# Input projection by one level of Strassen's products, all of it first, in a hybrid mLSTM and conformer block

## The chip, the cores and the metric

The kernel runs on one core of one Trainium2 chip. The metric is the device time of one execution in microseconds. The times of before are those of three runs; the profile is one further execution, recorded by the hardware profiler. PE is the matrix engine, DVE, ACT and POOL the vector, scalar and GpSimd engines, SP the engine that issues most transfers.

## The reference

One layer on x of 1024 tokens by 1024 channels, all in float32:

```
proj = rmsnorm(x) @ w_in                  # 1024 x 7168
xa, za, ub, gb, zb, g_a, g_b = split(proj)  # seven sections of 1024 channels
xc = silu(conv4(xa));  q, k = blockdiag(xc);  v = blockdiag(xa)
ha = standardize(mlstm_chunkwise(q, k, v, gates(q, k, v)))       # 4 heads
ya = ((ha * g + skip * xc) * silu(za)) @ w_proj
c  = conv31(ub * sigmoid(gb))             # causal, per channel
yb = (silu(layernorm(c)) * silu(zb)) @ w_pw2 + b
x  = x + (sigmoid(g_a) * ya + sigmoid(g_b) * yb) @ w_out
x  = x + (p @ w_ple) * sigmoid(rmsnorm(x) @ w_gate)
out = rmsnorm(x)
```

## The kernel before

All activations lie with channels on the 128 partitions and tokens along the free axis, in 8 channel tiles of 128x1024. A float32 product is made of three passes in the engine's float32r format: each operand is split exactly in a high part (a cast, L87, on ACT) and a low part (a subtraction, L88, mostly on DVE), and hi x hi, hi x lo and lo x hi are added up in PSUM. `gemm` (L208 to 222) makes one output tile of 128 channels by 1024 tokens: 8 input tiles by 2 halves of the tokens by 3 passes, 48 matmuls of 128x512. `gemm_half` does one half with 24.

The input projection has 56 output tiles, 8 in each of seven sections: XA (input of the first branch), ZA (its gate), UB and GB (input and gate of the long conv), ZB, GA and GBT. Before, these tiles are mixed with the rest: XA with the short conv and v, ZA with the four heads of the matrix memory, GA with the projection of the first branch, GBT and ZB beside the layer norm of the second branch; then follow pw2, the merge, `out` and `gate`. So long chains of small operations have whole GEMMs of other tiles beside them.

Weights come through the class `Stream` (L137 to 175): a raw load on SP, a cast on ACT, a subtraction on DVE. The raw buffer `wr` is single, the split parts are double; raw tiles of `out` and `gate` go to ordinary slots, of which there are 20.

The long conv has 31 taps of 128x1024, each one instruction on DVE (L347, L350), in SBUF. `drain(n)` hands out a few of them after each piece of other work, with the scheduling priority CONV_LATER.

The order on each engine is written down once, when the program is built: a scheduler takes the instructions by priority and by when it expects their inputs. On the chip each engine runs its list in order and waits where an input is missing.

Of the kernel before, what the change touches and what calls it, by code (L numbers as in the profile page):

```python
# [45 lines left out]
def block_kernel(ctx: ExitStack, tc: tile.TileContext, xT, pT, w_in, w_proj, w_pw2, w_out, w_ple,  # L46
# [12 lines left out]
    pm = ctx.enter_context(tc.tile_pool(name="pm", bufs=4, space=bass.MemoryType.PSUM))
    dp = ctx.enter_context(tc.tile_pool(name="dp", bufs=1, space=bass.MemoryType.DRAM))  # L60

    uid = [0]

    def slot(shape=(P, S), dt=F32, pool=None):
        uid[0] += 1
        pool = pool or sp
        full = pool.tile([P, NCK // 2 * DV], dt, tag="s", name=f"s{uid[0]}")
# [10 lines left out]
    def mbank(n=512):  # L78
        uid[0] += 1
        return pm.tile([P, 512], F32, tag="m", name=f"m{uid[0]}")[:, :n]  # L80

    def gbank():
        uid[0] += 1
        return pg.tile([P, S], F32, tag="g", name=f"g{uid[0]}")

    def split(src, hi, lo, eng=V):
        A.copy(out=hi, in_=src)  # L87
        eng.tensor_tensor(out=lo, in0=src, in1=hi.bitcast(F32), op=ALU.subtract)  # L88

# [9 lines left out]
    x_t = []  # L99
    for t in range(NT):  # L100
        xt = slot()
        nc.sync.dma_start(out=xt, in_=xT[t * P:(t + 1) * P, :])
        x_t.append(xt)
    pools = [vp, vp, vp, vp, zp, zp, zp, sp]
    parts = [slot(dt=F32R, pool=q) for q in pools]
# [19 lines left out]
    G.memset(eps_c, EPS)  # L125

# [4 lines left out]
    ple_d = dp.tile([NT, P, S], F32, name="ple_d")  # L131
    c_d = dp.tile([NT, P, S], F32, name="c_d")
    ma_d = dp.tile([NT, P, S], F32, name="ma_d")
    mrow_d = dp.tile([NH, S + NCK], F32, name="mrow_d")

# [43 lines left out]

    def plan(kind, *cts):  # L180
        order.extend((kind, t) for t in cts)

    def plan_pair(t):
        plan("in", GB + t, UB + t)

    for t in range(NT):
        plan("in", XA + t)
        if t in (1, 4):
            plan_pair(t // 4)
    for h in range(NH):  # L190
        plan("in", ZA + 2 * h, ZA + 2 * h + 1)
        plan_pair(2 + h)
    for t in range(NT):
        plan("in", GA + t)
        plan("proj", t)
        if t in (0, 2):
            plan_pair(6 + t // 2)
    plan("in", *range(GBT, GBT + NT))
    plan("in", *range(ZB, ZB + NT))
    plan("pw2", *range(NT))  # L200
    for kind in ("out", "gate"):
        plan(kind, *range(NT))
        plan(kind, *range(NT))
    srcs = {"in": w_in, "proj": w_proj, "pw2": w_pw2, "out": w_out, "gate": w_gate}
# [3 lines left out]
    def gemm(kind, ct, act_hi, act_lo):  # L208
        """[128 output channels, 1024 tokens] = w tile^T @ act; act_*(kt, half)."""
# [30 lines left out]
    def rstd_cols(ssum, n, out):  # L240
        """out = 1/sqrt(ssum/D + eps), [128, n]"""
        rt = sm.tile([P, NCK], F32, tag="rt", name=f"rt{uid[0]}")
        uid[0] += 1
        A.activation(rt[:, :n], ssum, AF.Sqrt, bias=eps_c, scale=1.0 / D)
        V.reciprocal(out=out, in_=rt[:, :n])

    def row_bcast(dst, rcol, n):
        """dst [128, n*128] = every partition the values of rcol [128, n], token-major"""
        for c in range(n):
            PE.matmul(dst[:, c * P:(c + 1) * P], rcol[:, c:c + 1].broadcast_to([P, P]), ident,  # L250
                      start=True, stop=True)

# [1 line left out]

    def ple_tile(ct):
        ps = gbank()
        cs = slice(ct * P, (ct + 1) * P)
        for h in range(2):
            for k in range(2):
                o = ps[:, h * HT:(h + 1) * HT]  # L260
                hs = slice(h * HT, (h + 1) * HT)
                PE.matmul(o, wple_s[k][0][:, cs], p_s[k][0][:, hs], start=k == 0, stop=False)
                PE.matmul(o, wple_s[k][0][:, cs], p_s[k][1][:, hs], start=False, stop=False)
                PE.matmul(o, wple_s[k][1][:, cs], p_s[k][0][:, hs], start=False, stop=k == 1)
        st = slot()
        A.copy(out=st, in_=ps)  # L266
        G.dma_start(out=ple_d[ct], in_=st)

# [1 line left out]
    xsq = slot()  # L270
    with tc.manual_schedule(engines={mybir.EngineType.Activation}):
        for t in range(NT):
            sq = xsq if t == 0 else slot()
            A.activation(sq, x_t[t], AF.Square)
            if t > 0:
                V.tensor_tensor(out=xsq, in0=xsq, in1=sq, op=ALU.add)
            if t % 2 == 1:
                ple_tile(t // 2)
    ssq = mbank(2 * NCK)
    for c in range(NCK):  # L280
        PE.matmul(ssq[:, 2 * c:2 * c + 2], xsq[:, c * P:(c + 1) * P], ones2, start=True, stop=True)
    rx = sm.tile([P, NCK], F32, tag="rc", name="rx")
    rstd_cols(ssq.rearrange("p (c w) -> p c w", w=2)[:, :, 0], NCK, rx)
    for _ in range(2):
        ws.load()
        ws.prep()

    h_hi = [hp.tile([P, NT, HT], F32R, tag="H", name=f"hhi{h}") for h in range(2)]
    h_lo = [hp.tile([P, NT, HT], F32R, tag="H", name=f"hlo{h}") for h in range(2)]
    rrow = [mbank() for _ in range(2)]  # L290
    for h in range(2):
        row_bcast(rrow[h], rx[:, 4 * h:4 * h + 4], 4)
    for t in range(NT):
        for h in range(2):
            x = x_t[t][:, h * HT:(h + 1) * HT]
            V.scalar_tensor_tensor(out=x, in0=x, scalar=vcol("norm_g", t), in1=rrow[h],  # L296
                                   op0=ALU.mult, op1=ALU.mult)
            split(x, h_hi[h][:, t], h_lo[h][:, t], G if h else V)
# [562 lines left out]
```

## Time and profile before

| | us |
|---|---|
| median of three runs | 1172.96 |
| lowest and highest | 1172.73, 1173.2 |
| span of the profiled execution | 1169.3 |
| PE busy in it | 1147.2 |
| DVE busy in it | 817.7 |
| ACT busy in it | 400.4 |
| POOL busy in it | 33.0 |

The profiled span leaves out some 3.7 us that lie around it in a timed run (1173.0 less 1169.3). Matmuls overlap in the engine, so the busy time of one (some 0.39 us) is longer than the distance from one to the next, which is read from the count in a stretch of time.

### The profile page before, as it was taken

The page shows a single profiled execution, that of the slowest core. Times are in us where ns is not written, and L with a number is a line of the kernel's source. Part 1 is how long each engine was busy: PE and PEld are TensorE (multiplying, and loading weights), DVE is VectorE, ACT ScalarE, POOL GpSimd, SP SyncE. Part 2 cuts the span into 40 slices and gives each one's busy share as a digit, 9 for nine tenths or more (in the row PEclk, how much of TensorE's full clock was granted, in tenths as well). Part 3 has the DMA queues.
Part 4 walks back from the last instruction along what each step waited for, and adds up shares of the span by engine and source line. Part 5 has one row for each costly group of instructions (what it writes and reads, how often), then busy time and mean ns, then how long its engine had stood idle before and what let it go on. Part 6 is the DMA issues. An engine that isn't in the chain of part 4 may idle for free.

```text
span 1169.3 us, 13098 instructions
## 1 busy us (share of the span) xinstructions
PE 1147.2 (98%) x5276; PEld 929.8 (80%) x5276; DVE 817.7 (70%) x1113; ACT 400.4 (34%) x540; POOL 33.0 (3%) x67
## 2 busy tenths in 40 slices
PE   7999999999999999999999999999999999999996
PEld 5777777778787887888888888888888888888885
DVE  5929989869984699828769999365334545466875
ACT  7633323642525343221111111147232212334542
POOL 1400000000000000000000000000000000000000
PEclk9999999999999999999999999999999999999998
DMA  9311121201011011221211233211113229422232
GB/s 328 133 36 36 38 72 36 71 20 55 19 62 47 19 55 37 72 91 42 102 54 55 108 105 112 90 54 36 55 36 108 90 73 387 152 87 94 91 127 72
DMA packets 29660, 98.18 MB, mean 84 GB/s; under 512 B 3148, under 2 KB 5340, under 8 KB 29600
## 3 DMA queue, kind: packets, MB, share of 16 engines
q1 hardware_dynamic: 25344, 82.37, 20.5%
q0 software_dynamic: 4256, 14.98, 3.3%
q8 instruction: 41, 0.67, 0.2%
q14 instruction: 19, 0.16, 0.0%
HBM read 80.55 MB, written 16.79 MB: 83 GB/s over the span
## 4 chain that ended last, share of the span: by engine, by line
PE 93%; DVE 4%; ACT 1%; DMA 1%; issue 0%; SPq 0%; DVEq 0%; ACTq 0%
PE g L221 21%; PE g L217 21%; PE g L218 21%; PE g L235 5%; PE g L234 5%; PE g L236 5%; PE m L548 2%; PE m L561 2%; PE m L535 1%; PE m L403 1%; PE m L555 1%; PE m L512 1%; DVE s L296 1%; PE m L594 1%; PE m L421 1%; PE m L250 1%
## 5 line engine op out<-in xcount | busy, mean ns | idle before, releaser
L217 PE MATMUL g<-hhi,wh 128*128 128x512 f32 x896 | 354.4, 396 | 0.5 <-ACT s L266 0.5
L218 PE MATMUL g<-hlo,wh 128*128 128x512 f32 x896 | 352.2, 393 | 0.4 <-POOL hlo L88 0.4
L350 DVE SCALAR_TENSOR_TENSOR s<-s,vecs,s 128x1023 f32<-128x1023 f32 (+15 forms) x240 | 300.5, 1265 | 4.3
L221 PE MATMUL g<-hhi,wl 128*128 128x512 f32 x896 | 283.0, 394 | 0.0
L87 ACT CAST wh<-wr 128x1024 fp32r<-128x1024 f32 x72 | 75.8, 1053 | 437.1 <-PE g L218 432.4
L221 PEld LDWEIGHTS g<-hhi,wl 128*128 128x128 f32 x896 | 167.7, 188 | 38.3 <-issue 4.5
L217 PEld LDWEIGHTS g<-hhi,wh 128*128 128x128 f32 x896 | 168.3, 188 | 37.2 <-issue 2.9
L218 PEld LDWEIGHTS g<-hlo,wh 128*128 128x128 f32 x896 | 168.3, 188 | 36.2 <-issue 1.8
L88 DVE TENSOR_TENSOR wl<-wr,wh 128x1024 fp32r<-128x1024 f32 x72 | 87.9, 1220 | 121.4 <-ACT wh L87 121.2
L217 PE MATMUL g<-s,wh 128*128 128x512 f32 x256 | 101.0, 395 | 0.0
L218 PE MATMUL g<-s,wh 128*128 128x512 f32 x256 | 100.8, 394 | 0.0
L221 PE MATMUL g<-s,wl 128*128 128x512 f32 x256 | 80.2, 394 | 0.0
L87 ACT CAST wh<-s 128x1024 fp32r<-128x1024 f32 x32 | 33.6, 1050 | 76.8 <-PE g L235 32.6
L218 PEld LDWEIGHTS g<-s,wh 128*128 128x128 f32 x256 | 48.1, 188 | 11.4
L217 PEld LDWEIGHTS g<-s,wh 128*128 128x128 f32 x256 | 48.1, 188 | 11.3
L221 PEld LDWEIGHTS g<-s,wl 128*128 128x128 f32 x256 | 48.1, 188 | 11.3
L235 PE MATMUL g<-nlo,wh 128*128 128x512 f32 (+1 forms) x136 | 51.5, 379 | 0.0
L234 PE MATMUL g<-nhi,wh 128*128 128x512 f32 (+1 forms) x136 | 51.3, 377 | 0.0
L236 PE MATMUL g<-nhi,wl 128*128 128x512 f32 (+1 forms) x136 | 51.2, 377 | 0.0
L88 DVE TENSOR_TENSOR wl<-s,wh 128x1024 fp32r<-128x1024 f32 x32 | 39.1, 1223 | 16.1 <-ACT wh L87 16.0
L235 PE MATMUL g<-mlo,wh 128*128 128x512 f32 x128 | 50.0, 391 | 0.0
L234 PE MATMUL g<-mhi,wh 128*128 128x512 f32 x128 | 49.8, 389 | 0.0
(193 smaller groups left out, 1340.7 us busy)
## 6 DMA issues: line engine op xcount, KB each, us to landing
wr<-in_w_in SPq DMA_DIRECT2D x56, 512.0 KB, 3.4
s<-in_xT SPq DMA_DIRECT2D x16, 512.0 KB, 9.1
s<-in_w_out SPq DMA_DIRECT2D x16, 512.0 KB, 10.1
s<-in_w_gate SPq DMA_DIRECT2D x16, 512.0 KB, 3.5
ple_d<-s POOLq DMA_DIRECT2D x8, 512.0 KB, 3.8
c_d<-s POOLq DMA_DIRECT2D x8, 512.0 KB, 2.9
wr<-in_w_proj SPq DMA_DIRECT2D x8, 512.0 KB, 3.4
s<-c_d SPq DMA_DIRECT2D x8, 512.0 KB, 4.0
```

What stands on the lines that cost most here:

```text
L87: A.copy(out=hi, in_=src)
L88: eng.tensor_tensor(out=lo, in0=src, in1=hi.bitcast(F32), op=ALU.subtract)
L217: PE.matmul(o, hi[:, kt], act_hi(kt, h), start=kt == 0, stop=False)
L218: PE.matmul(o, hi[:, kt], act_lo(kt, h), start=False, stop=False)
L221: PE.matmul(o, lo[:, kt], act_hi(kt, h), start=False, stop=kt == NT - 1)
L234: PE.matmul(ps, hi[:, kt], act_hi(kt)[:, qs], start=kt == 0, stop=False)
L235: PE.matmul(ps, hi[:, kt], act_lo(kt)[:, qs], start=False, stop=False)
L236: PE.matmul(ps, lo[:, kt], act_hi(kt)[:, qs], start=False, stop=kt == NT - 1)
L250: PE.matmul(dst[:, c * P:(c + 1) * P], rcol[:, c:c + 1].broadcast_to([P, P]), ident, start=True, stop=True)
L350: yield lambda d=d: V.scalar_tensor_tensor(out=c[:, d:], in0=ug[:, :S - d], scalar=vcol("conv_b_w", t, KB - 1 - d, KB), in1=c[:, d:], op0= ...
L548: PE.matmul(up, xn[:, i * P:(i + 1) * P], v, start=True, stop=True)
L561: PE.matmul(p2, qt[i][:, cs], X[:, i], start=i == 0, stop=i == 1)
```

## The change

The 28 pairs of output tiles of the input projection are computed first, in the order of `plan`. The first two pairs are plain. Of the others `pair_fast` makes four blocks of 128 channels by 512 tokens (two tiles, two halves of the tokens) with seven products over half of the input channels, in place of eight: 7 x 4 x 3 = 84 matmuls where there were 96. The sums of activations that this needs (F0 to F6) are made once. Those of the weights are made for each pair in `weights_fast` on POOL, where also the subtractions of the splits are now; its buffers are single. Four banks of PSUM, a to d, hold the products; `u` and `z` are sums of them on DVE, and three additions of L532 make three of the four blocks.

The results ZA, ZB, GA, GBT, xc, v and the conv are written to DRAM and read back later. The long conv adds up in PSUM (`pc`, one buffer), all taps are issued at once behind the UB pair with the old priority, and ACT copies the result to a slot that is taken behind the next UB tile's. The mean over channels comes from `csum`. After the last pair come the layer norm, the heads with two pw2 tiles behind each, proj with the merge, `out` and `gate`; `Stream` loads all its weights, `out` and `gate` too, to the single buffer `wr`, and POOL makes the low parts of pw2 and proj.

```diff
+    plan = [(GB, 0), (UB, 0), (XA, 0), (XA, 1), (XA, 2), (GB, 1), (UB, 1), (XA, 3), (ZB, 0), (ZB, 1),
+            (GB, 2), (UB, 2), (ZB, 2), (ZB, 3), (GBT, 0), (GB, 3), (UB, 3), (GBT, 1), (GBT, 2),
+            (GBT, 3), (GA, 0), (GA, 1), (GA, 2), (GA, 3), (ZA, 0), (ZA, 1), (ZA, 2), (ZA, 3)]
...
+    def weights_fast(n):
...
+            r0, r1 = wide("r0", NT, F32), wide("r1", NT + KH, F32)
+            nc.sync.dma_start(out=r0, in_=w_in[sec + 2 * j])
+            nc.sync.dma_start(out=r1[:, KH:], in_=w_in[sec + 2 * j + 1])
...
+            G.tensor_tensor(out=s3, in0=a21, in1=a11, op=ALU.subtract)
...
+            G.tensor_tensor(out=two(s21), in1=two(r1[:, :NT]),
...
+            G.tensor_tensor(out=s4, in0=a12, in1=s21[:, :KH], op=ALU.subtract)
+            w1 = wparts(r0, "w1")
+            w3 = wparts(s21, "w3")
+            w4 = wparts(s4, "w4", KH)
...
+            w2 = wparts(ends, "w2", view=two)
...
+    def pair_fast(ws):
...
+        a, b, c, d = bank(), bank(), bank(), bank()
+        u, z = temp(), temp()
+        product(a, w1, 0, 0)
+        A.copy(out=u, in_=a)
+        product(b, w3, 0, 4)
+        V.tensor_tensor(out=u, in0=u, in1=b, op=ALU.add)
+        product(a, w1, KH, 1, True)
+        yield 0, 0, a, None
+        product(d, w3, KH, 3)
+        V.tensor_tensor(out=z, in0=u, in1=d, op=ALU.add)
+        product(c, w2, 0, 5)
+        yield 1, 1, c, z
+        product(d, w4, 0, 2, True)
+        yield 0, 1, d, u
+        product(c, w2, KH, 6, True)
+        yield 1, 0, c, u
...
+    def long_conv(t, ug):
+        with tc.high_priority(offset=CONV_LATER):
+            c = new(pc, (P, S), tag="c")
+            V.tensor_scalar(out=c, in0=ug, scalar1=vcol("conv_b_w", t, KB - 1, KB),
+                            scalar2=vcol("conv_b_b", t), op0=ALU.mult, op1=ALU.add)
+            for d in range(1, KB):
+                V.scalar_tensor_tensor(out=c[:, d:], in0=ug[:, :S - d],
+                                       scalar=vcol("conv_b_w", t, KB - 1 - d, KB),
+                                       in1=c[:, d:], op0=ALU.mult, op1=ALU.add)
+            o = slot()
+            A.copy(out=o, in_=c)
...
+                V.tensor_tensor(out=csum, in0=csum, in1=c, op=ALU.add)
+            nc.sync.dma_start(out=c_d[t], in_=o)
...
+    def pair(n):
...
+        o = [slot(), slot()]
+        for i, h, ps, add in parts_:
+            dst = o[i][:, h * HT:(h + 1) * HT]
+            src = ps
+            if add is not None:
+                V.tensor_tensor(out=dst, in0=add, in1=ps, op=ALU.add)
+                src = dst
...
+    mean = new(pc, (P, S), tag="c")
...
+        V.tensor_tensor(out=c, in0=c, in1=mean, op=ALU.subtract)
+        sq = csq if t == 0 else slot()
+        A.activation(sq, c, AF.Square)
+        if t > 0:
+            V.tensor_tensor(out=csq, in0=csq, in1=sq, op=ALU.add)
...
-                if order[i][0] in ("out", "gate"):
-                    t = slot((P, NT, P))
-                else:
-                    t = wp.tile([P, NT, P], F32, tag="wr", name=f"wr{i}", bufs=1)
+                t = new(wq, (P, NT, P), tag="wr", bufs=1)
...
+        V.tensor_tensor(out=c, in0=c, in1=rln, op=ALU.mult)
+        A.activation(c, c, AF.Silu, scale=vcol("ln_b_g", t), bias=vcol("ln_b_b", t))
+        V.tensor_tensor(out=c, in0=c, in1=z, op=ALU.mult)
...
+    for t in range(NT):
+        second_act(t)
+    for h in range(NH):
+        head(h)
+        pw2_tile(2 * h)
+        pw2_tile(2 * h + 1)
```

How the lists of the engines change is seen at three places. First DVE before, in a stretch with little but the long conv (L350; L88 splits weights, L615 reads a GEMM of proj out of PSUM):

```order
L347 TENSOR_SCALAR s_4023<-s_3119,vecs 128x1024
L350 SCALAR_TENSOR_TENSOR s_4023<-s_3119,vecs,s_4023 128x1023
...
L350 SCALAR_TENSOR_TENSOR s_4023<-s_3119,vecs,s_4023 128x1017
L88 TENSOR_TENSOR wl_3968<-wr_3903,wh_3967 128x1024
L350 SCALAR_TENSOR_TENSOR s_4023<-s_3119,vecs,s_4023 128x1016
...
L350 SCALAR_TENSOR_TENSOR s_4023<-s_3119,vecs,s_4023 128x1010
L615 TENSOR_TENSOR s_3958<-g_3971,s_3958 128x1024
L88 TENSOR_TENSOR wl_4031<-wr_3965,wh_4030 128x1024
```

No more than seven taps stand together there or anywhere else in the list.

Next DVE after, in the last XA pair, which comes behind the second UB pair. L382 makes z of this pair, L399 is a tap of the long conv, c_1667 and c_1703 are the sums of its two tiles, L407 adds to csum, L532 makes the pair's own blocks:

```order
L382 TENSOR_TENSOR t_1771<-t_1770,b_1769 128x512
L399 SCALAR_TENSOR_TENSOR c_1667<-s_1565,vecs,c_1667 128x1016
...
L399 SCALAR_TENSOR_TENSOR c_1667<-s_1565,vecs,c_1667 128x994
L407 TENSOR_TENSOR s_501<-s_501,c_1667 128x1024
L396 TENSOR_SCALAR c_1703<-s_1566,vecs 128x1024
L399 SCALAR_TENSOR_TENSOR c_1703<-s_1566,vecs,c_1703 128x1023
...
L399 SCALAR_TENSOR_TENSOR c_1703<-s_1566,vecs,c_1703 128x994
L532 TENSOR_TENSOR s_1764<-t_1770,b_1769 128x512
L532 TENSOR_TENSOR s_1765<-t_1771,b_1768 128x512
```

Between L382 and the first L532 stand 23 and 30 taps, L407 and L396. The pairs behind the third and fourth UB pair have the same count; in the pair behind the first UB pair it is 16 and 30 taps.

Then PE after at the same place: b_1768 and b_1769 are the banks c and d of this pair, b_2025 and b_2026 the banks a and b of the next. L180 to L182 are the three passes:

```order
L182 MATMUL b_1768<-F5h_445,w2l_1562 128x512
L180 MATMUL b_1769<-F2h_301,w4h_1557 128x512
...
L182 MATMUL b_1769<-F2h_301,w4l_1558 128x512
L180 MATMUL b_2025<-F0h_297,w1h_1748 128x512
...
L182 MATMUL b_2025<-F1h_299,w1l_1749 128x512
L180 MATMUL b_2026<-F4h_443,w3h_1752 128x512
L434 MATMUL v_1872<-bvf_500,s_1764 128x136
L180 MATMUL b_1768<-F6h_832,w2h_1561 128x512
```

The second product into c (F6) stands behind both products into a of the next pair; the bank c is read by an L532 between its two products, and b_2026 takes over the bank of b_1769 when an L532 has read it.

## Rows read from the trace of the kernel before

**Rows 1.** Page, section 1: busy us (share of the span) xinstructions of each engine
```profile
PE 1147.2 (98%) x5276; PEld 929.8 (80%) x5276; DVE 817.7 (70%) x1113; ACT 400.4 (34%) x540; POOL 33.0 (3%) x67
```

**Rows 2.** Page, section 4: the chain that ended last, shares
```profile
PE 93%; DVE 4%; ACT 1%; DMA 1%; issue 0%; SPq 0%; DVEq 0%; ACTq 0%
PE g L221 21%; PE g L217 21%; PE g L218 21%; PE g L235 5%; PE g L234 5%; PE g L236 5%; PE m L548 2%; PE m L561 2%; PE m L535 1%; PE m L403 1%; PE m L555 1%; PE m L512 1%; DVE s L296 1%; PE m L594 1%; PE m L421 1%; PE m L250 1%
```

**Rows 3.** Windows: length, busy us (xinstructions) per engine, PEclk, DMA share, GB/s
```profile
core 0: us, PE busy (x) PEld busy (x) DVE busy (x) ACT busy (x) POOL busy (x), PEclk, DMA share, GB/s
...
600.00:700.00 100.00, 100.00 (x438) 81.77 (x437) 98.62 (x84) 14.10 (x14) 2.81 (x5) 1.00 0.24 83
...
900.00:1000.00 100.00, 100.00 (x435) 81.32 (x434) 47.01 (x63) 23.10 (x30) 0.00 (x0) 1.00 0.51 190
...
1150.00:1169.00 19.00, 8.15 (x59) 7.70 (x57) 11.21 (x27) 3.94 (x9) 0.00 (x0) 0.71 0.33 110
```

**Rows 4.** Waits of PE: what for, us in total, times, longest
```profile
PE g L262 <- ACT s L87: 6.7, 2, 6.5
```

**Rows 5.** Page, section 5: busy us, mean ns of one, idle before
```profile
L350 DVE SCALAR_TENSOR_TENSOR s<-s,vecs,s 128x1023 f32<-128x1023 f32 (+15 forms) x240 | 300.5, 1265 | 4.3
```

**Rows 6.** Groups by line and form, DVE, with one PSUM operand; last, tensor-scalar
```profile
L703 DVE SCALAR_TENSOR_TENSOR s<-g,vecs,s 128x512 f32<-128x512 f32 x16 | 12.0, 748 | 41.4 <-PE g L221 41.4
...
L676 DVE TENSOR_TENSOR s<-s,m 128x512 f32<-128x512 f32 x16 | 9.7, 679 | 0.6 <-PE m L250 0.6
...
L372 DVE TENSOR_TENSOR s<-g,s 128x1024 f32<-128x1024 f32 x8 | 9.7, 1216 | 30.7 <-PE g L221 30.7
...
L347 DVE TENSOR_SCALAR s<-s,vecs 128x1024 f32<-128x1024 f32 x8 | 6.5, 808 | 0.0
```

**Rows 7.** Timeline of DVE: start us, length, line, operation, xcount
```profile
532.25 0.81 DVE L347 TENSOR_SCALAR s<-s,vecs 128x1024 f32<-128x1024 f32 x1
533.10 9.18 DVE L350 SCALAR_TENSOR_TENSOR s<-s,vecs,s 128x1023 f32<-128x1023 f32 x7
542.20 1.22 DVE L88 TENSOR_TENSOR wl<-wr,wh 128x1024 fp32r<-128x1024 f32 x1
```

**Rows 8.** Groups by line and form: splits, casts and a square
```profile
L88 DVE TENSOR_TENSOR wl<-wr,wh 128x1024 fp32r<-128x1024 f32 x72 | 87.9, 1220 | 121.4 <-ACT wh L87 121.2 <-issue 0.2
...
L87 ACT CAST wh<-wr 128x1024 fp32r<-128x1024 f32 x72 | 75.8, 1053 | 437.1 <-PE g L218 432.4 <-issue 3.8 <-ACT s L677 0.8
...
L88 POOL TENSOR_TENSOR hlo<-s,hhi 128x512 fp32r<-128x512 f32 x8 | 12.2, 1533 | 2.4 <-ACT hhi L87 2.4
...
L654 ACT ACTIVATE s<-s 128x1024 f32<-128x1024 f32 x8 | 8.5, 1063 | 8.8 <-DVE s L652 8.3
```

**Rows 9.** Timeline of POOL: splits of h
```profile
34.12 4.76 POOL L88 TENSOR_TENSOR hlo<-s,hhi 128x512 fp32r<-128x512 f32 x3 [0.72 <-ACT hhi L87]
39.16 1.68 POOL L88 TENSOR_TENSOR hlo<-s,hhi 128x512 fp32r<-128x512 f32 x1 [0.28 <-ACT hhi L87]
...
47.72 1.28 POOL L88 TENSOR_TENSOR hlo<-s,hhi 128x512 fp32r<-128x512 f32 x1 [0.24 <-ACT hhi L87]
```

**Rows 10.** Timeline of DVE while POOL splits h, and just before
```profile
36.66 1.08 DVE L88 TENSOR_TENSOR hlo<-s,hhi 128x512 fp32r<-128x512 f32 x1
...
38.98 0.68 DVE L88 TENSOR_TENSOR hlo<-s,hhi 128x512 fp32r<-128x512 f32 x1
39.58 0.74 DVE L296 SCALAR_TENSOR_TENSOR s<-s,vecs,m 128x512 f32<-128x512 f32 x1
```

**Rows 11.** Page, section 6, DMA: xcount, KB each, us to landing
```profile
wr<-in_w_in SPq DMA_DIRECT2D x56, 512.0 KB, 3.4
...
s<-in_w_out SPq DMA_DIRECT2D x16, 512.0 KB, 10.1
...
s<-c_d SPq DMA_DIRECT2D x8, 512.0 KB, 4.0
```

**Rows 12.** Groups by line and form: the short conv
```profile
L389 DVE SCALAR_TENSOR_TENSOR s<-s,vecs,s 128x1022 f32<-128x1022 f32 x8 | 10.3, 1284 | 0.0
```

More of the change, by code (lines that the diff above doesn't have):

```diff
@@ L59, in block_kernel, with new @@
[L59 to L67, printed above, removed]
+    uid = [0]
+    def new(pool, shape, dt=F32, tag="s", **kw):
+        uid[0] += 1
+        return pool.tile(list(shape), dt, tag=tag, name=f"{tag}{uid[0]}", **kw)
@@ L76, in slot, with bank, vbank, temp @@
         return t
[L78 to L88, printed above, removed]
+    def bank(n=HT):
+        return new(pa, (P, HT), tag="b")[:, :n]
+    def vbank(n=HT):
+        return new(pv, (P, HT), tag="v")[:, :n]
+    def temp(n=HT):
+        return new(tp, (P, HT), tag="t")[:, :n]
     ident = cp.tile([P, P], F32, name="ident")
     nc.sync.dma_start(out=ident, in_=cst[:, 0:P])
-    pT_r, wple_r = [slot() for _ in range(2)], [slot() for _ in range(2)]
+    start = ExitStack()
+    st = pool_of(start, "st", 12, side="right")
+    def early(dt=F32):
+        return new(st, (P, S), dt, tag="q")
+    pT_r, wple_r = [early() for _ in range(2)], [early() for _ in range(2)]
     for h in range(2):
@@ L98, in block_kernel @@
             nc.sync.dma_start(out=pT_r[k][:, hs], in_=pT[k * P:(k + 1) * P, hs])
[L99 to L105, printed above, removed]
+    x_t = [None] * NT
+    for t in (0, 4, 1, 5, 2, 6, 3, 7):
+        x_t[t] = slot()
+        nc.sync.dma_start(out=x_t[t], in_=xT[t * P:(t + 1) * P, :])
+    parts = [early(F32R) for _ in range(8)]
     wple_s, p_s = [parts[0:2], parts[2:4]], [parts[4:6], parts[6:8]]
@@ L129, in vcol, with rstd_cols, row_bcast @@
         return vecs[:, o:o + 1]
[L131 to L134, printed above, removed]
+    def rstd_cols(ssum, n, out):
+        uid[0] += 1
+        rt = cp.tile([P, NCK], F32, tag="rt", name=f"rt{uid[0]}")
+        A.activation(rt[:, :n], ssum, AF.Sqrt, bias=eps_c, scale=1.0 / D)
+        V.reciprocal(out=out, in_=rt[:, :n])
+    def row_bcast(dst, rcol, n):
+        for c in range(n):
+            PE.matmul(dst[:, c * P:(c + 1) * P], rcol[:, c:c + 1].broadcast_to([P, P]), ident,
+                      start=True, stop=True)
@@ new lines, in block_kernel @@
+    xsq = early()
+    with tc.manual_schedule(engines={mybir.EngineType.Activation}):
+        for n, t in enumerate((0, 4, 1, 5, 2, 6, 3, 7)):
+            sq = xsq if n == 0 else early()
+            A.activation(sq, x_t[t], AF.Square)
+            if n > 0:
+                V.tensor_tensor(out=xsq, in0=xsq, in1=sq, op=ALU.add)
+            if n % 2 == 1:
+                ple_tile(n // 2)
+    ssq = vbank(2 * NCK)
+    col_sums(ssq, xsq, NCK)
+    rx = cp.tile([P, NCK], F32, name="rx")
+    rstd_cols(ssq.rearrange("p (c w) -> p c w", w=2)[:, :, 0], NCK, rx)
@@ new lines, in block_kernel @@
+    for ct in range(4, NT):
+        ple_tile(ct)
+    start.close()
+    fb = pool_of(one, "fb", 1, side="right", reuse_waits="tile")
+    t1, t2, t3 = [form(i, fb) for i in (3, 4, 5)]
+    for k in range(KH):
+        (a0, a1), (b0, b1) = halves(k), halves(k + KH)
+        s1, s2 = temp(), temp()
+        V.tensor_tensor(out=s1, in0=a1, in1=a0, op=ALU.subtract)
+        V.tensor_tensor(out=s2, in0=b1, in1=s1, op=ALU.subtract)
+        V.tensor_tensor(out=a1, in0=a1, in1=b1, op=ALU.subtract)
+        V.tensor_tensor(out=b0, in0=b0, in1=s2, op=ALU.subtract)
+        for s, f in ((s1, t1), (s2, t2), (a1, t3)):
+            split(s, f[0][:, k], f[1][:, k], G)
@@ new lines, in pair_fast, with product @@
+    def pair_fast(ws):
+        w1, w2, w3, w4 = ws
+        def product(o, w, k0, f, more=False):
+            for k in range(KH):
+                mm3(o, [q[:, k0 + k] for q in w], [q[:, k] for q in F[f]], k == 0 and not more,
+                    k == KH - 1, more)
+        a, b, c, d = bank(), bank(), bank(), bank()
[14 more added lines that the diff above has]
+        yield 1, 0, c, u
@@ new lines, in block_kernel @@
+    for n in range(len(plan)):
+        if n + 1 >= PLAIN and n + 1 < len(plan):
+            ready[n + 1] = weights_fast(n + 1)
+        pair(n)
+        if n == 0:
+            small_maps()
+        if n == 1:
+            form_t4()
+        if plan[n] == (XA, 3):
+            gates()
+    mean = new(pc, (P, S), tag="c")
+    for h in range(2):
+        PE.matmul(mean[:, h * HT:(h + 1) * HT], meanw, csum[:, h * HT:(h + 1) * HT], start=True, stop=True)
+    csq = slot()
+    for t in range(NT):
+        c = slot()
+        nc.sync.dma_start(out=c, in_=c_d[t])
+        V.tensor_tensor(out=c, in0=c, in1=mean, op=ALU.subtract)
[3 more added lines that the diff above has]
+            V.tensor_tensor(out=csq, in0=csq, in1=sq, op=ALU.add)
+        nc.sync.dma_start(out=cm_d[t], in_=c)
@@ L159, in prep @@
                 raw = self.raw.pop(i)
-                hi = wp.tile([P, NT, P], F32R, tag="wh", name=f"wh{i}")
-                lo = wp.tile([P, NT, P], F32R, tag="wl", name=f"wl{i}")
-                split(raw, hi, lo)
+                hi = new(wq, (P, NT, P), F32R, tag="wh")
+                lo = new(wq, (P, NT, P), F32R, tag="wl")
+                split(raw, hi, lo, V if order[i][0] in ("out", "gate") else G)
                 self.ready[i] = (hi, lo)
@@ L178, in block_kernel @@
     order = []
[L180 to L204, printed above, removed]
+    for kind in ("pw2", "proj", "out", "out", "gate", "gate"):
+        order.extend((kind, t) for t in range(NT))
+    srcs = {"proj": w_proj, "pw2": w_pw2, "out": w_out, "gate": w_gate}
     ws.add([srcs[n][t] for n, t in order])
@@ L238, in gemm_half @@
         return out
[L240 to L267, printed above, removed]
@@ L270, in block_kernel @@
[L270 to L281, printed above, removed]
@@ L282, in block_kernel @@
[L282 to L298, printed above, removed]
@@ L516, in head @@
         for k in range(2):
+            sz = [half() for _ in range(2)]
+            for i in range(2):
+                nc.sync.dma_start(out=sz[i], in_=za_d[2 * h + i][:, k * HT:(k + 1) * HT])
             hn = slot((P, NCK // 2, DV))
```

668 lines of the change are left out of this document (373 added, 295 removed).

## The prediction

> **What bounds the kernel now.** I read the engines' busy times first: PE is busy for 98% of the span, DVE for 70%, ACT for 34%, POOL for 3% [rows 1]. The chain of waits says the same, 93% of it is PE and 63% the three lines of `gemm` [rows 2]. The windows give the price of a matmul: from 900 to 1000 us PE is never idle and issues 435, which is 0.230 us each [rows 3]. The longest wait of PE is 6.5 us, at the start [rows 4]. So time is saved where matmuls go, and lost where PE is made to wait. What the rows of DVE show is the other half: from 600 to 700 us DVE is 98.6 us busy, nearly all of it long conv, and PE does not wait at all [rows 3]. Those 300.5 us of taps [rows 5] are free because no more than seven stand together: seven take 9.1 us (533.10 to 542.20) before DVE turns to what a GEMM needs [rows 7], while one GEMM of 48 matmuls lasts 11.0 us.
>
> **What goes.** 26 pairs lose 12 matmuls each: 312 x 0.230 = 71.7 us of PE, all on the path. DVE loses the subtractions of 56 weight tiles, 56 x 1.22 = 68 us [rows 8]; it was not the bound, so I count nothing for that.
>
> **The long conv in front of the adds.** This is the large term. A fast pair needs DVE inside its own chain: bank c is read by L532 between its two products, and the next pair's b takes over the bank of d once L532 has read that. In the list of DVE both tiles of the long conv stand between L382 and these two L532. The next pair's products into a still run, then PE has nothing it may do. Count from the end of the first product into d. PE has c (12 matmuls), the second into d (12) and the two into a (24): 48 x 0.230 = 11.0 us. DVE has L382 (0.7), 23 + 30 taps, L407 (1.2, as L372 [rows 6]), L396 (0.8) and L532 twice (0.7 each, as L676 [rows 6]). A chained tap takes 1.30 us from start to start, 9.10/7 [rows 7], so the taps take 53 x 1.30 = 68.9 and the whole 73.0 us. PE stands still for 62 us, in the pairs behind the second, third and fourth UB pair: 186. Behind the first there are 46 taps: 59.8 + 4.1 = 63.9, less 11.0 gives 53. Sum 239 us.
>
> No row shows a tap that adds up in PSUM. From below I take L372, 1.22 for 1024 elements with one operand in PSUM; from above twice L703, 2 x 0.748 = 1.50 for two halves [rows 6]. With 205 taps in the four bursts that is 222 to 280 us. I take 1.30, since L372 and the SBUF tap lie side by side and the chained step adds a little. Neither is near the 0.17 us (9 us for 53) at which PE would cover a burst. DVE cannot pass over a tap, so nothing hides this; ACT and POOL get ahead meanwhile, which cheapens the next terms.
>
> **POOL's loop.** Per pair POOL does 5632 elements per partition, 11 times 512. Its eight splits of h took 1.53 us each on average, 1.28 when alone [rows 8, 9]: 14.1 to 16.8 us, and 18.5 if each were as slow as the 1.68 of one of them [rows 9]. The raw load of r1 (3.4 us [rows 11]) lies between w2's split and the next s3, since both buffers are single. So 17.5 to 20.2 us a pair against 84 x 0.230 = 19.3 of PE. I take 5 us in all; ends 0 and 26 x 1 = 26, and more only if every split is slow (a rival below).
>
> The Trainium skill (GPSIMD Engine Reference, 4.1 Engine selection) says to put a two-input elementwise operation on VectorE, since GpSimd is about twice as slow. By it a pair would cost 5.5 x 2 x 1.22 = 13.4 us of POOL, and the loop would stay hidden. The rows with 1.53 per 512 give a ratio nearer 2.2 against DVE's 0.68, so here the trace is the harsher, and the sum above goes by it.
>
> **Start.** Seven forms F in place of two, 8 + 12 + 8 POOL splits or DVE ones before the fast pairs are served, and weights of pair 2 in the same queue: some 5 more operations of 1.5 us than the two plain pairs (44 us) cover. I take 7 us, ends 0 and 20.
>
> **XA pairs and gates.** In four pairs DVE has two short convs more, each 0.8 (a tensor-scalar as L347 [rows 6]) and 3 x 1.28 [rows 12], 4.6 us, in front of the next pair's adds, where only 12 matmuls (2.8 us) are between the products of one bank. DVE operations with two SBUF operands are slower while POOL works, 1.08 against 0.68, those with a PSUM operand are not, 0.74 [rows 10]. Per pair 4 us: 15 in all, ends 0 and 30. The gates' chain falls on DVE and ACT in the pair behind them: 8, ends 0 and 15.
>
> **Between the projection and the heads.** Before, the layer norm lay beside GBT and ZB tiles. Now, behind the last product, DVE has 8 subtractions and 7 additions of 1.22 us (18.3), a root, a reciprocal and eight small matmuls (5), then 16 multiplications of 1.22 (19.5) and one for the mask, all ahead of the first chunk of head 0. PE has only the four matmuls of q, some 2.5 us. 40 us; ends 20 (if the scheduler's list lets some of the first 15 run early) and 50.
>
> **Heads, proj.** Each head has two pw2 tiles (22 us) as cover; before it had four tiles. I take 10, ends -5 and 30.
>
> **out and gate.** Before, their raw tiles came far ahead: 10.1 us from issue to landing did not matter [rows 11]. Now the one buffer `wr` makes load, cast and subtraction one loop, 3.4 + 1.05 + 1.22 and some 0.4 of handing over, 6.1 us against 24 x 0.230 = 5.5 for half a tile. 32 x 0.6 = 19; I take 20, ends 0 and 35.
>
> **Sum.** From the profiled execution, 1169.3 and 3.7 around it, 1173.0, which is the median shown: - 71.7 + 239 + 5 + 7 + 15 + 8 + 40 + 10 + 20 = 1445 us.
>
> **The clock.** In the idle tail, where PE is 8.15 of 19 us busy, the granted clock is 0.71; in the two full stretches it is 1.00 [rows 3]. Four waits of 53 to 62 us are longer than any in this trace, so PE may come back at the lower level. If a whole pair ran at half the clock after each, that would be 4 x 19.3 = 77 us more. That is an end of the range, not a term. The Trainium skill (TensorE: Matmul & The Clock Gate, What's actually happening) has it as a rule that an idle array falls to 1.2 GHz and activity gives 2.4 GHz back; the tail agrees in kind, and how long the return takes here no row shows.
>
> **Rivals.** *Only the saving counts.* The bursts do not hold PE, because the scheduler's list leaves PE something or the taps are quick; then 1173 - 72 + 15 to 60 for the rest: 1115 to 1160, faster. It needs a tap below 0.2 us or a PE that doesn't wait for L532; the lists speak against both. 7 in 100. *POOL binds every pair.* With 1.68 us per 512 elements the loop is 18.5 + 3.4 and some 0.5 of handing over, 22.4 us, 3.1 over PE's 19.3, in the 18 or so pairs that no burst gives a lead: 56 more, 1501. For it speaks that POOL beside DVE is slow in the rows, against it that the two-operand taps which slowed it now have one operand in PSUM. 12 in 100. *The clock stays down after each burst:* 1445 + 77 = 1522, 6 in 100. *The saving does not come*, because the additions on DVE bound every pair and not only those behind UB: five of 0.7 are 3.5 us of 19.3 and each has 12 matmuls or more before its result is needed, so at most 26 x 2.8 = 73 more, 1518: 4 in 100. *Small terms at their low ends*, with bursts of 222: 1173 - 72 + 222 + 15 = 1338, and with a part of the taps done earlier than listed against PE, some 1290: inside the forecast's range.
>
> **Numbers.** My forecast, slower by the bursts, has 70 in 100: 1445, itself 1300 to 1530. The upper rivals lie inside this. The faster rival holds 7, 1 is left for no change, within 0.2%, which is what a measurement of this kernel tells from nothing; slower has 92. The range is 1300 to 1530.
>
> **What would show it.** PE near 1076 us busy, with four gaps of 50 to 65 us, each ended by L532 on DVE, and DVE in each in an unbroken run of L399 at about 1.30 us. A gap of some 40 us at L568 to L782; in `out` and `gate` short waits every 5.5 us for a cast or split of weights; POOL near 26 x 15 to 17 us and more. I am wrong if the runs of L399 stand beside a busy PE, if a tap is far from 1.3 us, or if waits for POOL's low parts come to more than 50 us.

## The result and the profile after

The changed kernel takes 1532.7 us (median of four runs, 1530.0 to 1533.6) against 1173.1 in the runs beside it: 1.307 times as long, with a 95% interval of 1.305 to 1.308. The forecast was slower, 1445 us, with a range of 1300 to 1530. The direction and the largest term came as worked out; the time is 88 us longer than the sum and lies just beyond the range. In the last experiment below one execution, 1486.2 us at a granted clock of 0.733 where its others had 0.939 to 0.942, was in a slower state of the chip and is left out.

The page's busy times, answering [rows 1]:

```profile
PE 1135.0 (74%) x4964; PEld 891.3 (58%) x4964; DVE 908.2 (59%) x1151; ACT 464.2 (30%) x661; POOL 483.4 (32%) x268
```

PE is busy nearly as long as before with 312 matmuls fewer, and idle for 393 us where it was idle for 22. What it waited for (us in total, times, longest), answering [rows 4]:

```profile
PE b L180 <- DVE s L532: 250.6, 5, 63.2
PE v L176 <- DVE s L577: 44.4, 1, 44.4
PE m L755 <- DMA x<-xc_d: 28.1, 3, 27.5
PE v L434 <- DVE gv L442: 13.4, 7, 3.6
PE b L180 <- ACT q L60: 8.2, 2, 6.1
PE b L180 <- ACT s L535: 7.3, 2, 6.1
...
PE b L182 <- POOL w3l L211: 4.6, 1, 4.6
...
PE g L689 <- ACT wh L60: 1.2, 1, 1.2
```

Three lines hold most of it. 250.6 us are waits for L532, the adds behind the long conv; 44.4 and 27.5 us are single waits, both between the projection and the heads. For a cast of weights in `out` and `gate`, the last line, PE waits 1.2 us.

One of the four bursts, in the timeline of DVE (start us, length, line, operation, count), answering [rows 7]:

```profile
308.72 0.68 DVE L382 TENSOR_TENSOR t<-t,b 128x512 f32<-128x512 f32 x1
309.32 29.96 DVE L399 SCALAR_TENSOR_TENSOR c<-s,vecs,c 128x1016 f32<-128x1016 f32 x23
340.37 1.22 DVE L407 TENSOR_TENSOR s<-s,c 128x1024 f32<-128x1024 f32 x1 [1.08 <-ACT s L403]
341.62 1.35 DVE L396 TENSOR_SCALAR c<-s,vecs 128x1024 f32<-128x1024 f32 x1
343.00 39.22 DVE L399 SCALAR_TENSOR_TENSOR c<-s,vecs,c 128x1023 f32<-128x1023 f32 x30
382.13 1.28 DVE L532 TENSOR_TENSOR s<-t,b 128x512 f32<-128x512 f32 x2
```

The 23 and 30 taps stand between L382 and L532 as in the list. 29.96 us for 23 is 1.303 us a tap, the 1.30 of the prediction. PE in the same stretch:

```profile
319.24 0.39 PE L182 MATMUL b<-F1h,w1l 128*128 128x512 f32 x1
382.87 0.80 PE L180 MATMUL b<-F4h,w3h 128*128 128x512 f32 x1 [63.24 <-DVE s L532]
...
384.86 0.63 PE L181 MATMUL b<-F6l,w2h 128*128 128x512 f32 x1
385.28 0.63 PE L182 MATMUL b<-F6h,w2l 128*128 128x512 f32 x1
...
388.00 0.40 PE L180 MATMUL b<-F6h,w2h 128*128 128x512 f32 x1
388.24 0.39 PE L181 MATMUL b<-F6l,w2h 128*128 128x512 f32 x1
```

PE finishes the products into bank a at 319.6 and waits 63.2 us for L532; forecast were 62. When it comes back its matmuls start 0.43 us apart, later 0.23 to 0.24. The windows after the first burst, which ends at 181 us, a stretch of the projection without a wait (640 to 660), and one in the middle of the handover show why (length, busy us and instructions of PE, its weight loads, DVE, ACT and POOL, then PEclk, DMA share, GB/s):

```profile
182.00:184.00 2.00, 1.97 (x6) 1.68 (x7) 1.99 (x3) 0.00 (x0) 0.00 (x0) 0.50 0.64 262
...
186.00:188.00 2.00, 2.00 (x12) 1.74 (x11) 1.12 (x3) 0.95 (x1) 0.00 (x0) 0.93 0.00 0
188.00:190.00 2.00, 2.00 (x12) 1.67 (x11) 1.33 (x3) 1.97 (x5) 1.82 (x1) 1.00 0.00 0
...
640.00:660.00 20.00, 20.00 (x88) 16.35 (x87) 12.67 (x13) 4.38 (x5) 13.39 (x7) 1.00 0.18 60
...
955.00:980.00 25.00, 0.00 (x0) 0.00 (x0) 10.92 (x9) 6.13 (x6) 0.00 (x0) 0.50 0.54 189
```

PEclk is 0.50, the lower level of 1.2 GHz, while PE waits and for the first matmuls behind the wait; from 188 us on it is 1.00, 2.4 GHz. Summed over the whole span in steps of 1 us, busy time at the lower level costs 30.9 us, before 1.1.

The costliest groups of DVE, PE and POOL, answering [rows 5, 8] (busy us, mean ns of one, idle before):

```profile
L399 DVE SCALAR_TENSOR_TENSOR c<-s,vecs,c 128x1023 f32<-128x1023 f32 (+14 forms) x240 | 305.4, 1272 | 7.9
L180 PE MATMUL b<-F4h,w3h 128*128 128x512 f32 x104 | 44.1, 424 | 242.7 <-DVE s L532 242.7
L211 POOL TENSOR_TENSOR w2l<-r,w2h 128x1024 fp32r<-128x1024 f32 x27 | 66.7, 2470 | 331.6 <-ACT w2h L210 331.6
```

A tap that adds up in PSUM takes 1272 ns, in SBUF it took 1265. Of the 250.6 us, 242.7 stand in front of the first product into b, which are the four bursts. POOL's split of 1024 elements takes 2.47 us, less than twice the 1.53 of its 512 before.

The second place is the handover. SP's list there, and the first three operations of DVE that wait for it:

```profile
937.14 0.32 SPq L578 DMA_DIRECT2D cm_d<-s  x1
937.56 0.38 SPq L572 DMA_DIRECT2D s<-c_d  x1
943.08 0.32 SPq L578 DMA_DIRECT2D cm_d<-s  x1
943.45 0.42 SPq L572 DMA_DIRECT2D s<-c_d  x1
```

```profile
941.83 1.22 DVE L573 TENSOR_TENSOR s<-s,c 128x1024 f32<-128x1024 f32 x1 [4.71 <-DMA s<-c_d]
944.22 1.23 DVE L577 TENSOR_TENSOR s<-s,s 128x1024 f32<-128x1024 f32 x1 [1.17 <-ACT s L575]
947.55 1.22 DVE L573 TENSOR_TENSOR s<-s,c 128x1024 f32<-128x1024 f32 x1 [2.11 <-DMA s<-c_d]
```

Each load of c_d (L572) stands on SP behind the store of the tile before (L578), which waits for DVE's L573. So one tile takes 5.9 us (943.45 less 937.56), where the prediction had two operations of DVE, 2.4 us.

### The profile page after: what moved, and what is told of

Read it like the earlier page. It is cut to its first block, busy times and chain, and to the rows that moved or that the text cites. A ratio compares the mean times of both kernels' runs of the same rounds, so it can differ in the third digit from the quotient of the medians.

```text
span 1528.2 us, 13317 instructions
## 1 busy us (share of the span) xinstructions
PE 1135.0 (74%) x4964; PEld 891.3 (58%) x4964; DVE 908.2 (59%) x1151; ACT 464.2 (30%) x661; POOL 483.4 (32%) x268
## 5 line engine op out<-in xcount | busy, mean ns | idle before, releaser
L399 DVE SCALAR_TENSOR_TENSOR c<-s,vecs,c 128x1023 f32<-128x1023 f32 (+14 forms) x240 | 305.4, 1272 | 7.9
L180 PE MATMUL b<-F4h,w3h 128*128 128x512 f32 x104 | 44.1, 424 | 242.7 <-DVE s L532 242.7
L211 POOL TENSOR_TENSOR w2l<-r,w2h 128x1024 fp32r<-128x1024 f32 x27 | 66.7, 2470 | 331.6 <-ACT w2h L210 331.6
L180 PEld LDWEIGHTS b<-F4h,w3h 128*128 128x128 f32 x104 | 20.5, 197 | 248.6 <-DVE s L532 244.4
L532 DVE TENSOR_TENSOR s<-t,b 128x512 f32<-128x512 f32 x78 | 53.2, 686 | 125.0 <-PE b L182 124.9
L211 POOL TENSOR_TENSOR w1l<-r,w1h 128x1024 fp32r<-128x1024 f32 x26 | 62.4, 2399 | 48.1 <-ACT w1h L210 48.1
L237 POOL TENSOR_TENSOR z<-r 128x1024 f32<-128x1024 f32 x26 | 64.4, 2478 | 2.0
L382 DVE TENSOR_TENSOR t<-t,b 128x512 f32<-128x512 f32 x26 | 17.8, 686 | 79.2 <-PE b L182 79.2
L211 POOL TENSOR_TENSOR w3l<-z,w3h 128x1024 fp32r<-128x1024 f32 x26 | 62.4, 2399 | 1.3 <-ACT w3h L210 1.3
L61 DVE TENSOR_TENSOR wl<-wr,wh 128x1024 fp32r<-128x1024 f32 x32 | 39.2, 1225 | 32.4 <-ACT wh L60 32.4
L180 PE MATMUL b<-F6h,w2h 128*128 128x512 f32 x108 | 46.4, 429 | 9.1 <-DVE s L532 7.9
L673 PE MATMUL g<-wlo,wh 128*128 128x512 f32 x128 | 52.6, 411 | 0.0
L672 PE MATMUL g<-whi,wh 128*128 128x512 f32 x128 | 52.6, 411 | 0.0
L673 PE MATMUL g<-x,wh 128*128 128x512 f32 x128 | 50.9, 397 | 1.7 <-POOL x L772 1.7
```

The lines of the kernel that those rows point to most:

```text
L180: PE.matmul(o, w[0], x[0], start=start, stop=False, skip_group_check=more)
L211: eng.tensor_tensor(out=l, in0=src, in1=h.bitcast(F32), op=ALU.subtract)
L237: G.tensor_tensor(out=two(s21), in1=two(r1[:, :NT]), in0=a22.rearrange("p k c -> p (k c)").unsqueeze(1).broadcast_to([P, 2, HT]), op=ALU.add)
L399: V.scalar_tensor_tensor(out=c[:, d:], in0=ug[:, :S - d], scalar=vcol("conv_b_w", t, KB - 1 - d, KB), in1=c[:, d:], op0=ALU.mult, op1=ALU.add)
L532: V.tensor_tensor(out=dst, in0=add, in1=ps, op=ALU.add)
L672: PE.matmul(o, hi[:, kt], act_hi(kt, h), start=kt == 0, stop=False)
```

## The experiments

All times are medians; before took 1172.5 to 1173.0 us beside them.

**e1, the conv's sums in SBUF.**

```diff
-            c = new(pc, (P, S), tag="c")
+            c = slot()
...
-            o = slot()
-            A.copy(out=o, in_=c)
...
-            nc.sync.dma_start(out=c_d[t], in_=o)
+            nc.sync.dma_start(out=c_d[t], in_=c)
```

> The changed kernel with the long conv's sums in an SBUF slot in place of the single PSUM buffer, no copy by ACT; nothing else is changed. In its list of DVE two to four taps stand together, but for one run of 23 in the first XA pair behind the first UB pair. Theory A (the bursts of taps in front of the adds of the pair cost four waits, 250 us, and PE then comes back at the lower clock): waits of PE for L532 (now L530) fall from 250 to about 30 us, the low clock loses 10 to 15 us less, the time is about 1285 us (1265 to 1310). Rival B (taps with both operands in SBUF and POOL's weight sums stand in each other's way, and POOL becomes the bound of every pair): POOL's operations of 128x1024 go from 2.40 us to 4 or more, PE waits for POOL in most pairs, 1380 to 1520 us. Rival C (the waits only move to another place of DVE, since its work in the projection is the same): 1450 to 1530 us.

Measured: 1450.0 us, ratio 1.238 (1.236 to 1.240). Its taps and POOL's split of w1 (busy us, mean ns), then the largest of PE's waits:

```profile
L399 DVE SCALAR_TENSOR_TENSOR s<-s,vecs,s 128x1023 f32<-128x1023 f32 (+24 forms) x240 | 439.9, 1862 | 1.3
...
L211 POOL TENSOR_TENSOR w1l<-r,w1h 128x1024 fp32r<-128x1024 f32 x26 | 80.1, 3081 | 26.9 <-ACT w1h L210 26.9
```

```profile
PE b L180 <- DVE t L382: 85.2, 12, 10.8
```

The bursts are gone from the list and yet only 83 us come back. A tap now takes 1862 ns and POOL's split of w1 3081, against 1272 and 2399 in the changed kernel. 240 taps of 0.59 us more are 142 us of DVE, which is then busy for 1037.7 us and is what PE waits for, at L382 above all. PE is idle for 290 us in place of 393, but busy time at the lower clock costs 54 us in place of 31: the many shorter waits that are left cost more of it than the bursts did, where theory A expected 10 to 15 us less. Theory A's number failed. Rival B had the mechanism, though PE waits for DVE and not for POOL, and rival C the size. The Trainium skill (SBUF — State Buffer, Who interferes with whom; Summary: rules for kernel authors) states that a DVE instruction with two inputs in SBUF contends with a GpSimd instruction that reads SBUF, and that the second one to issue waits until the first has finished; by that rule the PSUM sums of the change keep the taps out of POOL's way, and the two pairs of numbers agree.

**e2, the handover's order on SP.**

```diff
-        nc.sync.dma_start(out=cm_d[t], in_=c)
+        nc.gpsimd.dma_start(out=cm_d[t], in_=c)
...
-        nc.sync.dma_start(out=z, in_=zb_d[t])
+        nc.gpsimd.dma_start(out=z, in_=zb_d[t])
```

> The changed kernel with the stores of c less mean (cm_d) and the loads of zb_d issued from POOL's queue in place of SP's; the conv as in the changed kernel. Theory A (between the projection and the heads each load of c_d stands on SP behind a store that waits for DVE, and the loads for head 0 behind loads of zb_d that wait for a slot): the wait of PE for L577 falls from 44 to about 24 us and that for xc_d from 27.5 to about 22; 1505 us (1495 to 1515). Rival (the chain of DVE and ACT is itself that long, the loads only seem to be waited for): 1528 to 1535 us.

Measured: 1518.6 us, ratio 1.297 (1.293 to 1.301). The waits of PE at the two halves of the handover:

```profile
PE v L176 <- DVE s L577: 30.5, 1, 30.5
PE m L780 <- ACT s L756: 26.9, 1, 26.9
```

The wait for L577 fell from 44.4 to 30.5 us, which is the whole gain of 14; theory A had 20 there and 5 more in the second wait, so its 1505 us was missed. The second wait did not shorten: it is now charged to L756, ACT's copies of q, in place of the transfer of xc_d. So the order on SP was shown as a cause of the first half. What holds the second half this run does not separate: in its trace ACT's copies stand behind the second branch's work, and DVE is busy with that without a break from 986 to 1004 us.

**e3, both edits.** It joins the diffs of e1 and e2.

> Both edits, conv in SBUF and the transfers between projection and heads from POOL's queue. Theory A: the gains add up, about 1260 us (1235 to 1285). If the waits hide one another, the gain is that of the conv alone, 1285 us.

Measured: 1435.5 us (1.222 to 1.227). The gains of 83 and 14 us add up to 97, as theory A has it; its 1260 us was missed because the gain of e1 was.

**e4, the copy's slot asked for earlier.**

```diff
+            o = slot()
             c = new(pc, (P, S), tag="c")
...
-            o = slot()
             A.copy(out=o, in_=c)
```

> The changed kernel with the slot for ACT's copy of the conv taken ahead of the taps, PSUM buffer as it is. Theory A (it is the single PSUM buffer c that puts the second tile's taps in front of the next pair's adds): the bursts stay, 1525 to 1540 us. Rival D (it is the slot of the copy): the bursts go, below 1350 us.

One run, 1528.2 us. PE's wait for the adds:

```profile
PE b L180 <- DVE s L532: 250.8, 5, 63.2
```

The bursts stayed, as theory A has it. The next run shows that theory A was wrong all the same.

**e5, a pool of its own for the copy.**

```diff
-    sp = pool_of(one, "sp", 9)
+    sp = pool_of(one, "sp", 8)
+    cq = pool_of(one, "cq", 1)
...
-            o = slot()
+            o = new(cq, (P, S), tag="co")
```

> The changed kernel with the slot for ACT's copy of the conv in a pool of its own (one buffer; the common slots go from nine to eight); the sums stay in the one PSUM buffer. In the list of DVE the three bursts of 53 taps are gone, two to four taps stand together, and one run of 16 is left behind the first UB pair. Theory A' (the common slots are handed out in the order of first use, so a tile of the next pair comes behind the copy and with it behind the taps; taps with one operand in PSUM don't disturb POOL): waits of PE for L532 fall from 250 to about 15 us, a tap stays near 1.27 us and POOL's 128x1024 near 2.4 to 2.5, about 1275 us (1255 to 1300). Rival B' (DVE is too full for the taps wherever their sums lie, the waits move to L382 and L378 as with the sums in SBUF): 1380 to 1450 us.

Measured: 1277.6 us, ratio 1.090 (1.088 to 1.091). The conv's group (L400 here) and w2's split on POOL (L212), then the waits of PE at the two halves of the handover and for the adds (L533 here):

```profile
L400 DVE SCALAR_TENSOR_TENSOR c<-s,vecs,c 128x1023 f32<-128x1023 f32 (+14 forms) x240 | 304.6, 1269 | 4.5
L212 POOL TENSOR_TENSOR w2l<-r,w2h 128x1024 fp32r<-128x1024 f32 x27 | 67.8, 2512 | 100.9 <-ACT w2h L211 100.8
```

```profile
PE v L177 <- DVE s L578: 43.9, 1, 43.9
PE m L756 <- DMA x<-xc_d: 29.4, 4, 27.9
...
PE b L181 <- DVE s L533: 8.4, 2, 7.9
```

The single PSUM buffer is still there and the bursts are gone: 255 us come back, the wait for the adds falls from 250.6 to 8.4 us. Taps (1269 ns) and POOL (2512) stay as fast as in the changed kernel, so the same 240 taps fit under the matmuls when they are spread and their sums lie in PSUM.

**e6, e5 with the edit of e2.**

> The run before with the stores of cm_d and the loads of zb_d from POOL's queue. Theory: the 14 us of the same edit on the changed kernel come again, about 1262 us (1245 to 1285). If the gain there belonged to the clock after the bursts, no difference.

Measured: 1261.6 us, ratio 1.076 (1.074 to 1.077): 16 us less than e5, much as the 14 on the changed kernel.

**e7, the layer norm's sums between the last pairs.** It builds on e5.

```diff
+        if n == 21:
+            ln_mean()
+        if 21 < n <= 21 + 4:
+            ln_tile(2 * (n - 21 - 1))
+            ln_tile(2 * (n - 21 - 1) + 1)
+        if n == 21 + 5:
+            ln_rstd()
...
-        nc.sync.dma_start(out=z, in_=zb_d[t])
+        nc.gpsimd.dma_start(out=z, in_=zb_d[t])
```

> The copy's own pool, and the layer norm's sums (mean, c less mean, squares) two tiles at a time behind the last pairs of the projection in place of behind all of them; zb_d is loaded from POOL's queue. Theory (44 us of wait for L577 are hidden under the pairs, the second half of the handover stays): about 1232 us (1215 to 1255), still slower than before, since start, XA pairs, gates, second half of the handover and heads keep some 130 us. Rival (the transfers and adds of the layer norm delay the pairs by as much): 1262 to 1275 us.

Measured: 1242.4 us, ratio 1.059 (1.057 to 1.061). The longest waits of PE:

```profile
PE m L770 <- DMA x<-xc_d: 23.9, 4, 21.9
PE m L795 <- ACT s L771: 17.2, 1, 17.2
```

The wait of 43.9 us is gone; with the loads of zb_d on POOL's queue that is 35 us of time. The second half, 21.9 and 17.2 us, is all still there.

**e8 and e9, the second half.** e8 is e7 with the row of the scale left in PSUM, e9 is e7 with the splits ahead of the heads on DVE.

```diff
-    rln = slot()
-    for k in range(2):
...
-        A.copy(out=rln[:, k * HT:(k + 1) * HT], in_=rp)
+    rln = gbank()
+    row_bcast(rln, rl, NCK)
```

```diff
-        split(c, w_hi[t // KH][:, t % KH], w_lo[t // KH][:, t % KH], G)
+        split(c, w_hi[t // KH][:, t % KH], w_lo[t // KH][:, t % KH], V)
```

> e7 with the row of the layer norm's scale left in PSUM in place of copied to SBUF, so that the eight multiplications by it ahead of the heads have one operand in SBUF in place of two. Theory (DVE operations with both operands in SBUF wait for POOL's split that runs beside them): these multiplications go from up to 3.3 us to 1.2 us each, the handover gets 8 to 12 us shorter, about 1232 us (1226 to 1239). Rival (DVE waits there for ACT and transfers): no difference, 1238 to 1246 us.

> e7 with the eight splits of the second branch's activations on DVE in place of POOL. Theory as in the run before: DVE has 8 more operations of 1.22 us and none of its 16 is held up by POOL; 24 x 1.22 = 29 us where it took 33, so 1237 us (1231 to 1245). Rival (DVE's list is the chain there and its operations take what they take): 10 us longer, 1250 us or more.

Measured: e8 1243.4 us (1.059 to 1.063), e9 1237.9 (1.053 to 1.058). The eight multiplications by the row of the scale and the eight by the gate, in e7 and then in e8 (busy us, mean ns):

```profile
L723 DVE TENSOR_TENSOR s<-s,s 128x1024 f32<-128x1024 f32 x8 | 18.1, 2296 | 0.1
L725 DVE TENSOR_TENSOR s<-s,v 128x1024 f32<-128x1024 f32 x8 | 12.9, 1650 | 0.8 <-ACT s L724 0.8
```

```profile
L720 DVE TENSOR_TENSOR s<-s,g 128x1024 f32<-128x1024 f32 x8 | 9.7, 1213 | 9.3 <-DMA s<-cm_d 9.3
L722 DVE TENSOR_TENSOR s<-s,v 128x1024 f32<-128x1024 f32 x8 | 16.5, 2062 | 2.3 <-DMA v<-zb_d 2.3
```

In e8 the multiplications by the row take 1.21 us each, as expected. But those by the gate, which still have both operands in SBUF, go from 1.65 to 2.06 beside POOL, so DVE wins only 5 us in all, and the time does not move. Only e9 takes the contention away: all 16 take 1.22 us. The waits of PE in e9:

```profile
PE m L770 <- DMA x<-xc_d: 26.1, 5, 21.3
...
PE m L795 <- ACT s L771: 3.4, 1, 3.4
PE m L808 <- DMA v<-v_d: 3.3, 1, 3.3
```

The wait for ACT's copies of q falls from 17.2 to 3.4 us, and 3.3 for v come in. That is 11 us less in this half; 7 of them are left where `out` begins, and the time is 4.5 us below e7's, with intervals that overlap. So by the trace the contention holds part of the second wait, though the times alone do not show it. The first wait, for xc_d, stays: 21.9 and 21.3 us. On SP its load is issued behind eight of cm_d, and while PE waits the DMA engines are fully busy (e7, columns as in the windows above):

```profile
698.00:704.00 6.00, 0.00 (x0) 0.00 (x0) 0.67 (x1) 0.70 (x1) 0.00 (x0) 0.50 1.02 406
710.00:716.00 6.00, 0.00 (x0) 0.00 (x0) 6.00 (x4) 3.73 (x4) 5.38 (x4) 0.50 1.02 411
```

No run loads xc_d ahead of cm_d, so what that would give is not shown.

**e10, the copy's slot used early.**

```diff
+            o = slot()
+            V.memset(o[:, :1], 0.0)
             c = new(pc, (P, S), tag="c")
...
-            o = slot()
             A.copy(out=o, in_=c)
```

> The changed kernel with the slot of ACT's copy asked for ahead of the taps, as in e4, and one column of it set to zero there, so that its first use comes ahead of the taps; slots common (nine), sums in the one PSUM buffer. Theory (common slots come in the order of first use): the three bursts of 53 taps go, as with the own pool, 1270 to 1290 us. Rival (the copy must not share its pool with the pairs' tiles, whenever it is first used): bursts stay, 1525 to 1540 us.

Measured: 1284.7 us, ratio 1.096 (1.094 to 1.098). PE's wait for the adds (L533 here):

```profile
PE b L180 <- DVE s L533: 1.5, 2, 0.9
```

Common slots, one PSUM buffer, and the bursts are gone. e10 differs from e4 only by the write of one column, and e5 from the changed kernel only by the pool, with one common slot fewer. So it is the first use of a slot in a shared pool that places the bursts, not the line that asks for it. The rule behind this, that the scheduler hands out the slots of one pool in the order of their first use in the program, is inferred from these runs. The slot of ACT's copy is first used behind the last tap, and the tiles of the next pair come behind it in the same pool; so their adds stand behind all the taps.

No version beats the kernel before. The best, e9, is 65 us slower.

## Why the prediction was wrong in its size

| term | forecast us | measured us |
|---|---|---|
| 312 matmuls less | -71.7 | 5276 to 4964 matmuls |
| four bursts | 239 | 242.7 |
| POOL's loop | 5 | 6.6 (waits for w3l and F6l) |
| XA pairs, gates | 23 | 13.4 and 11.0 |
| start | 7 | 17.5, of which 8 were there before |
| handover | 40 | 79.3 idle |
| heads, proj | 10 | 5 idle |
| out and gate | 20 | 10 (span of both stages, 204.6 against 194.8) |
| lower clock | 0, 77 as an end | 30 |
| other busy time of PE | 0 | 30 |

The terms are not all of one kind: idle time of PE, spans, and busy time that the sum did not have. Together idle time grew by 371 us, where the terms of waiting had 344; `out` and `gate`, where PE was idle for some 2 us in place of 20, hide part of the 39 by which the handover went over. Some 30 us each for the lower clock and for other busy time make up the rest of the 88.

**The bursts** were read rightly from the list, priced rightly, and they are seven tenths of the loss: 255 of 360 us come back in e5. What the prediction did not have is why they stand there; its reasons needed none, but a repair does. One premise was off without harm: the kernel before has runs of eight taps too, not only of seven (10.31 us from 630.61 on), still less than the 11.0 us of a GEMM.

**The handover** is the step that failed first. It counted DVE's 15 and 16 operations and took 40 us with 50 as an end; PE was idle for 79.3. SP's list was passed over: there every load waits behind a store that waits for DVE. e2 shows 14 us of it, e7 that 35 us can go under the pairs. The second half has 27.5 and 6 us of wait against the 20 counted; DVE's multiplications took 1.2 to 3.4 us each instead of 1.22, beside POOL's splits; the prediction had priced this slowing in the XA pairs and not here. On SP the load of xc_d stood until 1007.7 us behind loads of zb_d that waited for a buffer. e2 freed that load and the half stayed as long; e9, built on e7, freed the multiplications and 11 us of waits went. How much each holds in the changed kernel stays open.

**The clock** was put as an end of the range and left out of the sum. 30 us more are lost at the lower level than before. The prediction tied it to the bursts, and there it is small: in the 20 us or so behind each, some 10 us in all. The rest lies behind shorter waits, some 6 us of it in the first 180 us and 8 in the handover, and is there in e5 too, which still loses 26.7 us. Such waits had no price in the sum: the term was put at nothing, for want of a row. The Trainium skill (TensorE: Matmul & The Clock Gate, What's actually happening) says that an idle array falls to 1.2 GHz and that activity releases it; the windows after the burst agree, and the return came within some ten matmuls there, not a pair of tiles.

**Other busy time.** The busy time of PE less the low clock and the removed matmuls is 30 us higher than before (1104.1 against 1074.4). Two groups that were side by side with GEMM work before show up to 14 us of it, v's matmuls 23.5 against 17.9 and the gates' 16.4 against 8.3, part of which may be the lower clock again. In `out` and `gate` a matmul starts 0.234 us behind the one before, where it was 0.227 (medians of the starts), some 5 us more for the same 792 matmuls. Why, and where the rest lies, stays open.

**Out and gate** were overpriced: by its parts the loop of load, cast and subtraction takes 6.1 us a half tile, and yet PE waited only 2.3 us there for weights. Neither that nor the 10 us by which the two stages are still longer was tested; these 10 lie in part in the two rows below theirs.

**The rivals.** POOL never bound a pair in the changed kernel (6.6 us of waits). Its seven operations take 13.7 us a pair by their means (2.47 for w2's split), below the 14.1 to 16.8 of the prediction and near the 13.4 that it worked out from a factor of two and set aside. The saving did come: in e7, where nothing blocks the pairs, stretches of 20 us are wholly busy, and what is left of the loss, 73 us by the spans of the two profiled runs, is 100 us more idle time, 22 at the lower clock and 23 of other busy time, less 72 for the matmuls.

## What to carry to other kernels

Before a change that computes faster in one stage, read where its long side work stands in each engine's list, and on which queue each of its transfers waits: 312 matmuls less were worth 72 us, and what came with them cost some 430 (the loss of 360 and the 72), 255 of it for one buffer in a shared pool. If instructions of low priority stand in a block, look for a buffer that they share with the work behind them; its first use, not the line where it is asked for, may set the order. And count SP's list like an engine's wherever a loop stores and loads through one queue.

## What was not expected of the hardware

DVE operations with both operands in SBUF and POOL's two-operand operations slow each other down. With the taps spread over the pairs, a tap took 1862 ns with its sums in SBUF (e1) and 1269 with them in PSUM (e5); POOL's split of w1 took 3081 and 2489. Adding up in PSUM costs DVE no more than in SBUF: 1272 ns in the changed kernel against 1265 in the kernel before, where POOL was busy for 33 us only.
